# Weight sums later in VectorE's order, and the sixth down operand's difference in two parts

## The chip, the core and the metric

The kernel runs on one core of a Trainium2 chip. The time is device microseconds of one execution of the whole kernel, from inputs in HBM to the output in HBM. Five engines are named by their short names: PE (TensorE, matmuls), ACT (ScalarE), DVE (VectorE), POOL (GpSimd, here only an issuer of transfers that add to their destination) and SP (SyncE, here only an issuer of plain transfers). Every engine works through its own queue in order; they meet by semaphores.

## What is computed

A trunk of two macaron layers over 528 tokens (512 and 16 meta tokens), model width 1024, all in float32: a SwiGLU feed-forward at half weight, a mixer of gated linear attention beside grouped-query softmax attention, and a second feed-forward at half weight.

```python
def swiglu(x, w_gate, w_up, w_down):
    return (jax.nn.silu(x @ w_gate) * (x @ w_up)) @ w_down
...
    for l in range(DEPTH):
        h = h + 0.5 * swiglu(rmsnorm(h, norm_gains[l, 0]), ffn_w_gate[l, 0], ffn_w_up[l, 0], ffn_w_down[l, 0])
        h = h + mixer(rmsnorm(h, norm_gains[l, 1]), ...)
        h = h + 0.5 * swiglu(rmsnorm(h, norm_gains[l, 2]), ffn_w_gate[l, 1], ffn_w_up[l, 1], ffn_w_down[l, 1])
    return rmsnorm(h, final_norm)[:, N_META:]
```

The hidden width of the feed-forward is 2816, that is 22 tiles of 128, or 11 pairs of tiles. The change touches only the feed-forwards, of which there are four ("blocks" in the prediction).

## The kernel before

**Precision.** Every product of float32 matrices is made of three: each operand is split into a rounded part (hi) and the rest (lo), and hi*hi, hi*lo and lo*hi are summed in PSUM. For a weight slab of 128x1024 ACT makes `whi` (L287) and DVE makes `wlo` (L288); both pools have four buffers, and a slab is made three uses ahead of PE.

**Seven products instead of eight.** The feed-forward's matrices are cut in 2x2 blocks and multiplied by a Strassen-like scheme: the products "1", "2", "4" use a weight block as it lies in HBM ("11", "12", "22"), and "7", "6", "5", "3" use sums of blocks. Where a sum's two terms are both in HBM, POOL makes it by an adding transfer (L208). For the pairs from 2 to 10, DVE makes three: "7" is block 21 less block 11 (L244, in place in the tile of 21), "6" is block 22 plus "7" (L253, in place in the tile of 22), and "3" is "6" less block 12 (L256, the tile s4). Blocks "11", "12", "22" live in `wraw` (three buffers, tag raw), the sums in `wsa` and `wsb` (three each). Method `sums` issues these right after the slab of the product that it is called for has been made; `make` calls it for the products "1", "2" and "6".

**Pairs and groups.** `ffn_steps` writes out the order of the products. The 11 pairs form groups of 4, 4 and 3. The first two groups' down projection is fast too: its operands are sums of the hidden values of the group's four pairs, and its weight blocks count as pairs 11 to 14 ("quads"). When a group's last pair is nearly done, the step ("O", g, 0) makes operands "1", "2", "5" of the three finished pairs (`ks` = 0 to 2) and, after the last pair, ("O", g, 1) makes the same for pair 3 of the group and then operand "6" of all four. An operand is a hi part (ACT, L669) and a lo part (DVE, L670); a difference of hidden values (DVE, L674) comes first for "5" and "6". Operands "5" and "6" lie in the tiles tagged c, the others in g.

**Order.** The program is written in one order, and a scheduler then sets each engine's own order from readiness by its own costs. So a line that moves in the program may or may not move in an engine's queue. L614, L621 and L638 are the DVE steps that turn a pair's products into gate and up values, L648 multiplies them to hidden values, L716 adds a fast down product to h. `product_of_pair` holds the PE matmuls of L594, `fast_down` those of L708.

Of the kernel before, what the change touches and what calls it, by code (L numbers as in the profile page):

```python
# [14 lines left out]
ALU = mybir.AluOpType  # L15
# [133 lines left out]
NPAIR = FF // P // 2  # L149
# [21 lines left out]
class Weights:  # L171
# [59 lines left out]
    def sums(self, f, i, product, w):  # L231


        got, V = self.summed, self.nc.vector
        if (f, i) in OPENING and product in "12":
            (self.begin_sums if product == "1" else self.first_sum)(f, i, *[w] * (product == "1"))
        if i < 2:
            if product == "2":
                s4 = self.negative(f, i, "s4", w)
                self.add(s4, got[f, i, "6"])  # L240
                got[f, i, "3"] = s4
        elif product == "1":
            if i < NPAIR:
                V.tensor_tensor(got[f, i, "7"], got[f, i, "7"], w, ALU.subtract)  # L244
            else:
                got[f, i, "7"] = self.negative(f, i, "s3", w)
                self.add(got[f, i, "7"], self.dram(f, i, "21"))
            if not i < NPAIR:
                self.add(got[f, i, "6"], got[f, i, "7"])
        elif product == "2":  # L250
            self.kept = w
            if i < NPAIR:
                V.tensor_tensor(got[f, i, "6"], got[f, i, "6"], got[f, i, "7"], ALU.add)  # L253
        elif product == "6":
            s4 = self.long.tile([P, SLAB], F32, tag="wsa", name=f"s4_{f[0]}{f[1]}_{i}")
            V.tensor_tensor(s4, w, self.kept, ALU.subtract)  # L256
            got[f, i, "3"] = s4
# [15 lines left out]
    def make(self, upto):  # L273
        nc = self.nc
        while self.made < min(upto, len(self.loads)):
            self.fetch(self.made + 1)
            s = self.made
            load = self.loads[s]
            w = self.raws.pop(s, None)
            if w is None:  # L280
                w = self.summed.pop(load)
            hi = self.hi_pool.tile([P, SLAB], F32R, tag="whi", name=f"whi{s}")
            lo = self.lo_pool.tile([P, SLAB], F32R, tag="wlo", name=f"wlo{s}")
            for a in np.split(np.arange(SLAB), 2 if s == 0 else 1):
                cs = slice(a[0], a[-1] + 1)
                with self.tc.issue_after(self.behind) if self.behind else nullcontext():
                    nc.scalar.copy(hi[:, cs], w[:, cs])  # L287
                nc.vector.tensor_tensor(lo[:, cs], w[:, cs], hi[:, cs].bitcast(F32), ALU.subtract)  # L288
            self.got[s] = (hi, lo)
            self.got.pop(s - 12, None)  # L290
            self.made += 1
            if not isinstance(load, int) and load[2] in "126":
                self.sums(*load, w)

    def use(self, j, ahead=AHEAD_MADE):
        self.make(j + ahead)
        self.fetch(j + AHEAD_FETCHED)
        return self.got[j]

    def next(self, name):  # L300
        t = PLAN[self.pos]
        assert t[1] == name, (t, name)
        s, c = divmod(COLUMN[self.pos], SLAB)
        self.pos += 1
        hi, lo = self.use(self.at[s])
        return hi[:, c : c + t[5]], lo[:, c : c + t[5]]
# [18 lines left out]
def build(tc, ctx, xt, wts, win, par, w2, const, umask, out):  # L325
    nc = tc.nc
    V, S, G, TE = nc.vector, nc.scalar, nc.gpsimd, nc.tensor
# [24 lines left out]
    def close_pools(pools):  # L352
        for n in reversed(pools):
            slots.pop(n).release()
# [28 lines left out]
    def h(c, cs=None):  # L383
        return hall[:, c, cs or slice(0, live[0])]
# [184 lines left out]
    def ffn(l, f, norm, done, following):  # L569

        x, rs, up, n = norm.x, None, None, live[0]
        w = n // 2
# [85 lines left out]
        def operand(g, c, ks=slice(0, 4)):  # L658

            src = raw[g][{"1": 0, "2": 2, "5": 0, "6": 0, "7": 1, "3": 3, "4": 2}[c]]  # L660
            if (g, c) not in sets:
                tag = "c" if c in "56" else "g"
                sets[g, c] = [quarter(tag, F32R) for _ in range(2)]
            hi, lo = [t[:, ks] for t in sets[g, c]]
            if c == "3":
                S.activation(hi, src[:, ks], AF.Copy, scale=-1.0)
                V.scalar_tensor_tensor(lo, src[:, ks], -1.0, hi.bitcast(F32), ALU.mult, ALU.subtract)
            else:
                S.copy(hi, src[:, ks])  # L669
                V.tensor_tensor(lo, src[:, ks], hi.bitcast(F32), ALU.subtract)  # L670

        def difference(g, into, a, b, ks=slice(0, 4)):
            r = raw[g]
            V.tensor_tensor(r[into][:, ks], r[a][:, ks], r[b][:, ks], ALU.subtract)  # L674

        def operands_of(g, ks, order):
            for c in order:
                if c == "5":
                    difference(g, 0, 1, 0, ks)
                operand(g, c, ks)  # L680
# [10 lines left out]
        def fast_down(g, dq, c, part):  # L691
            last = sum(GROUPS[: g + 1]) - 1
            kinds = ("ss", "s2") if last % 2 == 0 else ("s2", "ss")
            st = made.setdefault(("S", g, dq), {})
            where = {"2": "Y", "5": "Z", "3": "Z"}.get(c, "X")
            begin = c in "125"
            if part != 2:
                if begin:
                    st[where] = pair(kinds[{"Y": 0, "Z": 1, "X": dq}[where]] == "s2")
                st["w"] = st.get("w", {})  # L700
                st["w"][c] = W.op((l, f), NPAIR + QUADS * g + dq, c, ahead=AHEAD_MADE - 1)
            acc = st[where][:, :, :w]
            hi, lo = st["w"][c]
            xs = sets[g, c]
            for k in {1: range(3), 2: range(3, 4), 3: range(4)}[part]:
                for j in range(2):
                    for i, (a, b) in enumerate(((hi, 0), (hi, 1), (lo, 0))):
                        TE.matmul(acc[:, j], a[:, j, k], xs[b][:, k], start=bool(begin and k == 0 and i == 0),  # L708
                                  stop=k == 3 and i == 2, skip_group_check=not begin)
            if part == 1:  # L710
                return
            st["w"].pop(c)
            for m, q in {"1": [(0, 0)], "2": [(0, 0)], "5": [(1, 1)], "6": [(0, 1)], "3": [(0, 1)], "7": [(1, 1)],
                         "4": [(1, 0)]}[c]:
                to = hall[:, 4 * dq + m : 4 * dq + m + 3 : 2, q * w : (q + 1) * w]
                V.tensor_tensor(to, to, acc, ALU.add)  # L716
            if dq == 1:
                sets.pop((g, c))
            operands_behind(g, dq, c)
# [24 lines left out]
        for i, step in enumerate(steps):  # L744
            if step[0] == "P":
                if step[1:] == (0, "5") and norm.acc is None:
                    for c in range(KC):
                        norm.square(c)
                product_of_pair(*step[1:])
                if step[1:] == (0, "5"):  # L750
                    rs, up = norm.rs(True)
                    W.behind = prev_act[0]
                if step[1] in (2, 3) and step[2] in "6574":
                    m = next(risen)
                    V.scalar_tensor_tensor(h(m), h(m), -1.0, up, ALU.mult, ALU.mult)
                if i == last_op:
                    close_pools(norm.pools)
                    following()
            elif step[0] == "S":
                fast_down(*step[1:])  # L760
            elif step[0] == "O":
                g, last = step[1:]
                operands_of(g, slice(3, 4) if last else slice(0, 3), "215" if last else "125")
                if last:
                    difference(g, 0, 3, 0)
                    operand(g, "6")
            else:
                down(*step[1:])
# [515 lines left out]
    for l in range(DEPTH):  # L1284
        a, b, c = norms[3 * l : 3 * l + 3]
        ffn(l, 0, a, b.chunk, lambda: operand_pools(b, "x"))
        close_pools(bp.pop())
        mixer(l, b, c.chunk_of_pair, lambda: (operand_pools(c, "xc"), bp.append(block_pools())))
        if l < DEPTH - 1:
            d = norms[3 * l + 3]  # L1290
            ffn(l, 1, c, d.pair_of, lambda: operand_pools(d, "xc"))
        else:
            ffn(l, 1, c, None, lambda: None)
# [72 lines left out]
```

## Time and profile before

| | us |
|---|---|
| median of 3 runs | 2219.3 (2217.36 to 2219.31) |
| the profiled execution | 2218.53 |
| its span, first to last instruction | 2216.8 |
| PE, DVE, ACT busy | 2164.6, 1784.4, 1210.7 |

PE is busy for nearly all of the span, so the figures of the other engines matter only where PE waits for them. In the rows, `out<-in` are tile names without buffer numbers, `<-` in square brackets names what ended the idle time before an instruction, and `q` behind an engine's name (DVEq, SPq) is its sequencer. Two instructions of DVE in a row overlap a little, so a start-to-start distance is some 0.08 us shorter than the time shown for one.

### The profile page before, as it was taken

Reading aid. Unit: us, or ns where it says so; the run is one execution under the profiler, and the core shown is the slowest. Engines: PE = TensorE matmul, PEld = TensorE weight load, DVE = VectorE, ACT = ScalarE, POOL = GpSimd, SP = SyncE. Lnnn points to the kernel's source line nnn. Section 1 sums busy time; section 2 is a strip of 40 time slices with the busy share of each in tenths; the row PEclk is TensorE's granted clock in tenths of the full one; section 3 lists DMA queues with packets and bytes.
Section 4 is the critical chain, followed back from the end, with each engine's and each line's share of the span. In section 5 each row is a group of like instructions: output and inputs, shape, how many; then the busy total and the mean of one; then the engine's idle time right before and its main releaser. Section 6 shows DMA issues by size and latency. Waiting matters only on the chain.

```text
span 2216.8 us, 40090 instructions
## 1 busy us (share of the span) xinstructions
PE 2164.6 (98%) x16506; PEld 2070.7 (93%) x16506; DVE 1784.4 (80%) x2695; ACT 1210.7 (55%) x1779; POOL 101.5 (5%) x120
## 2 busy tenths in 40 slices
PE   7999999999999999999999999999999999999998
PEld 6899999989999999999999999999788888999997
DVE  7887978486886688888789879775879767997987
ACT  7444545354785555454575445553557836554543
POOL 1000000000000001000010000000000001000100
PEclk9999999999999999999999999999999999999999
DMA  9675753212113467666566757432121146776752
GB/s 278 172 199 165 190 158 101 86 48 67 48 39 118 116 168 200 190 184 187 158 162 187 207 159 194 143 110 77 48 82 53 42 135 153 196 200 180 191 161 67
DMA packets 87463, 311.41 MB, mean 140 GB/s; under 512 B 9712, under 2 KB 12144, under 8 KB 87280
## 3 DMA queue, kind: packets, MB, share of 16 engines
q1 hardware_dynamic: 68624, 245.53, 33.0%
q0 software_dynamic: 16704, 60.82, 15.6%
q8 instruction: 130, 2.13, 0.4%
q10 hardware_dynamic: 1952, 2.50, 0.3%
q14 instruction: 53, 0.43, 0.1%
HBM read 289.94 MB, written 2.10 MB: 132 GB/s over the span
## 4 chain that ended last, share of the span: by engine, by line
PE 79%; DVE 11%; ACT 3%; issue 2%; DMA 1%; DVEq 0%; POOL 0%; ACTq 0%; POOLq 0%
PE ss L594 36%; PE mm L461 13%; PE ss L708 11%; PE ss L461 10%; PE sm L461 2%; DVE wlo L288 2%; DVE g L674 1%; PE sm L1069 1%; PE ss L1044 1%; DVE h L716 1%; PE ss L467 1%; DMA w<-win 1%; PE sm L1085 1%; ACT t L440 1%; DVE c L670 1%
## 5 line engine op out<-in xcount | busy, mean ns | idle before, releaser
L594 PE MATMUL ss<-xc,whi 128*128 128x264 f32 (+1 forms) x4928 | 905.3, 285 | 15.6 <-ACT whi L287 7.6
L594 PEld LDWEIGHTS ss<-xc,whi 128*128 128x128 f32 x4928 | 765.3, 189 | 20.5 <-ACT c L598 8.4
L594 PE MATMUL ss<-xc,wlo 128*128 128x264 f32 (+1 forms) x2464 | 701.5, 285 | 8.8 <-DVE wlo L288 8.7
L594 PEld LDWEIGHTS ss<-xc,wlo 128*128 128x128 f32 x2464 | 465.4, 189 | 11.2 <-DVE wlo L288 11.0
L288 DVE TENSOR_TENSOR wlo<-w,whi 128x1024 fp32r<-128x1024 f32 (+1 forms) x337 | 408.0, 1217 | 64.1 <-ACT whi L287 63.9
L287 ACT CAST whi<-w 128x1024 fp32r<-128x1024 f32 (+1 forms) x337 | 349.4, 1048 | 175.2 <-PE ss L594 82.1
L461 PE MATMUL mm<-x,whi 128*128 128x264 f32 (+1 forms) x1712 | 384.8, 315 | 0.0
L461 PEld LDWEIGHTS mm<-x,whi 128*128 128x128 f32 x1712 | 278.4, 188 | 16.6 <-issue 1.0
L461 PE MATMUL mm<-x,wlo 128*128 128x264 f32 (+1 forms) x856 | 266.0, 315 | 0.0
L708 PE MATMUL ss<-g,whi 128*128 128x264 f32 (+1 forms) x1280 | 238.6, 285 | 1.5 <-ACT g L669 1.4
L287 ACT CAST whi<-raw 128x1024 fp32r<-128x1024 f32 x126 | 132.1, 1048 | 163.6 <-PE mm L461 102.8
L598 ACT COPY c<-ss 128x528 f32<-128x528 f32 (+1 forms) x132 | 78.4, 594 | 259.1 <-PE ss L594 259.1
L288 DVE TENSOR_TENSOR wlo<-raw,whi 128x1024 fp32r<-128x1024 f32 x126 | 153.9, 1221 | 59.2 <-ACT whi L287 58.4
L708 PEld LDWEIGHTS ss<-g,whi 128*128 128x128 f32 x1280 | 199.0, 189 | 2.1 <-ACT g L669 1.6
L708 PE MATMUL ss<-g,wlo 128*128 128x264 f32 (+1 forms) x640 | 181.7, 284 | 0.0
L461 PEld LDWEIGHTS mm<-x,wlo 128*128 128x128 f32 x856 | 159.5, 188 | 8.5 <-issue 0.7
L461 PE MATMUL ss<-g,whi 128*128 128x264 f32 (+2 forms) x900 | 166.2, 299 | 0.0
L461 PEld LDWEIGHTS ss<-g,whi 128*128 128x128 f32 x900 | 131.7, 188 | 5.3
L208 POOL DMA_DIRECT2D w<-win x60 | 52.8, 880 | 1580.1 <-DVE wlo L288 463.9
L708 PEld LDWEIGHTS ss<-g,wlo 128*128 128x128 f32 x640 | 120.9, 189 | 0.0
L440 ACT ACTIVATE c<-c 128x528 f32<-128x528 f32 (+1 forms) x88 | 56.5, 642 | 93.6 <-DVE c L638 89.3
L708 PE MATMUL ss<-c,whi 128*128 128x264 f32 (+1 forms) x512 | 100.3, 289 | 7.1 <-DVE c L670 6.6
(267 smaller groups left out, 3375.3 us busy)
## 6 DMA issues: line engine op xcount, KB each, us to landing
w<-win SPq DMA_DIRECT2D x335, 512.0 KB, 4.5
raw<-wts SPq DMA_DIRECT2D x126, 512.0 KB, 3.3
w<-win POOLq DMA_DIRECT2D x60, 512.0 KB, 7.5
s<-win POOLq DMA_DIRECT2D x24, 512.0 KB, 7.0
w<-s POOLq DMA_DIRECT2D x24, 512.0 KB, 5.6
s<-w POOLq DMA_DIRECT2D x8, 512.0 KB, 7.7
h<-xt SPq DMA_DIRECT2D x3, 528.0 KB, 7.1
out<-h ACTq DMA_DIRECT2D x4, 256.0 KB, 2.4
```

The lines of the kernel that those rows point to most:

```text
L208: self.nc.gpsimd.dma_start(t, src, accum_op=ALU.add)
L287: nc.scalar.copy(hi[:, cs], w[:, cs])
L288: nc.vector.tensor_tensor(lo[:, cs], w[:, cs], hi[:, cs].bitcast(F32), ALU.subtract)
L440: prev_act[0] = S.activation(*args, **kw).ins
L461: TE.matmul(acc.half[i][:width], lhs, rhs[:, acc.spans[i]], start=first, stop=last)
L467: TE.matmul(a, weights, x[:, hs], start=True, stop=True)
L594: TE.matmul(acc[:, j], a[:, j, k], b[:, at], start=bool(begin and k == 0 and i == 0), stop=k == len(x) - 1 and i == 2, skip_group_check=no ...
L598: W.behind = S.copy(part(st, q), acc).ins
L670: V.tensor_tensor(lo, src[:, ks], hi.bitcast(F32), ALU.subtract)
L674: V.tensor_tensor(r[into][:, ks], r[a][:, ks], r[b][:, ks], ALU.subtract)
L708: TE.matmul(acc[:, j], a[:, j, k], xs[b][:, k], start=bool(begin and k == 0 and i == 0), stop=k == 3 and i == 2, skip_group_check=not begin)
L716: V.tensor_tensor(to, to, acc, ALU.add)
```

## The change

Three edits. In `sums`, the subtraction for "7" is issued when product "2"'s slab has been made, no longer product "1"'s; block 11's tile is kept for it (`kept1`). The addition for "6" is issued in `make`, right before the slab of "6" is made. And the difference for operand "6" is made for the three finished pairs in step ("O", g, 0) and for the last pair alone in ("O", g, 1), where it was made for all four at once.

```diff
         elif product == "1":
             if i < NPAIR:
-                V.tensor_tensor(got[f, i, "7"], got[f, i, "7"], w, ALU.subtract)
+                self.kept1 = w
...
         elif product == "2":
             self.kept = w
             if i < NPAIR:
-                V.tensor_tensor(got[f, i, "6"], got[f, i, "6"], got[f, i, "7"], ALU.add)
+                V.tensor_tensor(got[f, i, "7"], got[f, i, "7"], self.kept1, ALU.subtract)
...
             if not isinstance(load, int) and load[2] in "126":
                 self.sums(*load, w)
+            after = self.loads[s + 1] if s + 1 < len(self.loads) else 0
+            if not isinstance(after, int) and after[2] == "6" and 2 <= after[1] < NPAIR:
+                s2, s3 = [self.summed[after[:2] + (c,)] for c in "67"]
+                nc.vector.tensor_tensor(s2, s2, s3, ALU.add)
...
                 g, last = step[1:]
-                operands_of(g, slice(3, 4) if last else slice(0, 3), "215" if last else "125")
+                ks = slice(3, 4) if last else slice(0, 3)
+                operands_of(g, ks, "215" if last else "125")
+                difference(g, 0, 3, 0, ks)
                 if last:
-                    difference(g, 0, 3, 0)
                     operand(g, "6")
```

What the engines' queues make of it is shown at three places. A name such as w21_01_4 is a weight tile: block 21, layer 0, feed-forward 1, pair 4; s4 and s3 are sums, whi and wlo a slab's parts, and the last number counts buffers. Line numbers of the kernel after the change are 4 or 5 higher below the edits (L678 is the difference that was L674, L674 then is the lo part that was L670).

DVE in the second block, from the first weight slab of quad 11 to the step L621 (L625) of the group's last pair, before:

```order
L288 TENSOR_TENSOR wlo189_10090<-w11_01_11_9874,whi189_10089 128x1024
L614 TENSOR_TENSOR c816_9868<-c816_9868,ss818_10046 128x2x264
L638 TENSOR_SCALAR c816_9868<-c816_9868,rs800_9426 128x264
L288 TENSOR_TENSOR wlo190_10127<-s4_01_3_9942,whi190_10126 128x1024
L288 TENSOR_TENSOR wlo191_10162<-w12_01_11_9944,whi191_10161 128x1024
L638 TENSOR_SCALAR c816_9868<-ss814_9835,rs800_9426 128x264
L256 TENSOR_TENSOR s4_01_11_10250<-w22_01_11_9876,w12_01_11_9944 128x1024
L648 TENSOR_TENSOR g806_9504<-c816_9868,ss814_9835 128x264
L648 TENSOR_TENSOR g807_9505<-c816_9868 128x264
L288 TENSOR_TENSOR wlo192_10184<-w21_01_11_9878,whi192_10183 128x1024
L670 TENSOR_TENSOR g822_10081<-g806_9504,g821_10080 128x264
L621 TENSOR_TENSOR c815_9867<-c815_9867,ss818_10046 128x2x264
```

and after:

```order
L678 TENSOR_TENSOR g804_9504<-g807_9507,g804_9504 128x792
L618 TENSOR_TENSOR c816_9869<-c816_9869,ss818_10048 128x2x264
L288 TENSOR_TENSOR wlo190_10130<-s4_01_3_9944,whi190_10129 128x1024
L642 TENSOR_SCALAR c816_9869<-c816_9869,rs800_9428 128x264
L288 TENSOR_TENSOR wlo191_10165<-w12_01_11_9946,whi191_10164 128x1024
L642 TENSOR_SCALAR c816_9869<-ss814_9836,rs800_9428 128x264
L288 TENSOR_TENSOR wlo192_10187<-w21_01_11_9879,whi192_10186 128x1024
L652 TENSOR_TENSOR g806_9506<-c816_9869,ss814_9836 128x264
L652 TENSOR_TENSOR g807_9507<-c816_9869 128x264
L256 TENSOR_TENSOR s4_01_11_10253<-w22_01_11_9877,w12_01_11_9946 128x1024
L674 TENSOR_TENSOR g822_10083<-g806_9506,g821_10082 128x264
L625 TENSOR_TENSOR c815_9868<-c815_9868,ss818_10048 128x2x264
```

The early part of the difference (792 columns) stands right behind wlo189 (not repeated), and the weight sum s4 has moved from ahead of wlo192 to behind it. Eleven rows below L621 the difference of 128x1056 is one of 128x264. The other seven groups show the same.

DVE at the pair that follows that group, before and after:

```order
L288 TENSOR_TENSOR wlo200_10478<-w11_01_4_10252,whi200_10477 128x1024
L244 TENSOR_TENSOR w21_01_4_10254<-w21_01_4_10254,w11_01_4_10252 128x1024
L716 TENSOR_TENSOR h_82<-h_82,ss825_10160 128x2x264
L288 TENSOR_TENSOR wlo201_10508<-w21_01_12_10017,whi201_10507 128x1024
L716 TENSOR_TENSOR h_82<-h_82,ss830_10312 128x2x264
L288 TENSOR_TENSOR wlo202_10540<-w12_01_4_10351,whi202_10539 128x1024
L253 TENSOR_TENSOR w22_01_4_10256<-w22_01_4_10256,w21_01_4_10254 128x1024
```

```order
L288 TENSOR_TENSOR wlo200_10481<-w11_01_4_10255,whi200_10480 128x1024
L720 TENSOR_TENSOR h_82<-h_82,ss825_10163 128x2x264
L288 TENSOR_TENSOR wlo201_10510<-w21_01_12_10019,whi201_10509 128x1024
L720 TENSOR_TENSOR h_82<-h_82,ss830_10315 128x2x264
L288 TENSOR_TENSOR wlo202_10542<-w12_01_4_10354,whi202_10541 128x1024
L253 TENSOR_TENSOR w21_01_4_10257<-w21_01_4_10257,w11_01_4_10255 128x1024
L297 TENSOR_TENSOR w22_01_4_10259<-w22_01_4_10259,w21_01_4_10257 128x1024
```

The subtraction (L244, now L253) has moved past two wlo and two additions to h; the addition (L253, now L297) has stayed. On SP the load of pair 5's block 11, which takes the buffer of pair 4's, has moved behind that of pair 5's block 22.

POOL's adding transfers at the first group of the first block, before:

```order
L208 DMA s3_00_11_1133<-win 128x1024
L208 DMA w22_00_11_916<-s3_00_11_1133 128x1024
L208 DMA w21_00_11_918<-win 128x1024
L208 DMA s3_00_12_1263<-win 128x1024
L208 DMA w22_00_12_1055<-s3_00_12_1263 128x1024
```

and after:

```order
L208 DMA s3_00_11_1134<-win 128x1024
L208 DMA w21_00_11_917<-win 128x1024
L208 DMA w22_00_11_915<-s3_00_11_1134 128x1024
L208 DMA s3_00_12_1264<-win 128x1024
L208 DMA w22_00_12_1055<-s3_00_12_1264 128x1024
```

The sum w21 of quad 11 has moved ahead of w22<-s3. In the other groups POOL's order is the same before and after.

## The prediction

> **What bounds the kernel now.** I read the page first, then the list of waits for TensorE (PE), then the chain of work that ended last at one of the eight places that the change touches, and VectorE's (DVE) timeline there.
>
> ```profile
> span 2216.8 us, 40090 instructions
> PE 2164.6 (98%) x16506; PEld 2070.7 (93%) x16506; DVE 1784.4 (80%) x2695; ACT 1210.7 (55%) x1779; POOL 101.5 (5%) x120
> ...
> PE ss L594 <- DVE wlo L288: 8.7, 8, 3.1
> ...
> PE ss L708 <- DVE c L670: 6.6, 8, 0.9
> ...
> PE ss L708 <- ACT g L669: 1.4, 1, 1.4
> ...
> PE ss L708 <- DVE wlo L288: 0.6, 1, 0.6
> ```
>
> PE is busy for 98% of the span, so time can only come from the few microseconds in which it waits (columns: us in total, times, longest). One line is this change's own: PE waits eight times, 0.9 us at most and 6.6 in all, for the low part of an operand in a c tile (L670). That is the sixth down operand, once for each of two groups in four feed-forward blocks.
>
> How such a wait comes about is in the chain at the place of the second block's first group. The timelines of PE, ACT (ScalarE) and DVE at the same place follow it.
>
> ```profile
> 867.13 2.94 PE ss L594 x24
> 870.09 0.71 DVE c L621
> ...
> 877.70 1.25 DVE g L674
> 878.96 1.23 DVE h L716 x2
> 880.18 1.24 DVE c L670
> ```
>
> ```profile
> 881.47 0.39 PE L708 MATMUL ss<-c,whi 128*128 128x264 f32 x1 [0.91 <-DVE c L670]
> ```
>
> ```profile
> 877.00 1.05 ACT L287 CAST whi<-s 128x1024 fp32r<-128x1024 f32 x1
> 879.04 1.08 ACT L669 CAST c<-g 128x1056 fp32r<-128x1056 f32 x1 [1.00 <-DVE g L674]
> ```
>
> ```profile
> 859.98 0.98 DVE L670 TENSOR_TENSOR c<-g,c 128x792 fp32r<-128x792 f32 x1
> 860.87 1.22 DVE L288 TENSOR_TENSOR wlo<-w,whi 128x1024 fp32r<-128x1024 f32 x1
> ...
> 870.09 0.70 DVE L621 TENSOR_TENSOR c<-c,ss 128x528 f32<-128x528 f32 x1 [1.01 <-PE ss L594]
> ```
>
> PE's product ends at 870.07 and lets DVE start at L621. From there DVE has work without a pause until the difference (L674, four pairs wide) at 877.70; ACT rounds it (879.04 to 880.12), DVE takes the rest of the rounding (L670), and PE, which was ready 0.91 us before, goes on at 881.47. Just ahead of L621, DVE had been idle for 1.01 us.
>
> **The change, part by part.** *The difference in two parts.* The widths and durations of L674 in all of the trace are these:
>
> ```profile
> L674 DVE TENSOR_TENSOR g<-g,g 128x1056 f32<-128x1056 f32 x18 | 22.6, 1254 | 0.2
> L674 DVE TENSOR_TENSOR g<-g,g 128x1024 f32<-128x1024 f32 x6 | 7.3, 1221 | 0.1
> L674 DVE TENSOR_TENSOR g<-g,g 128x792 f32<-128x792 f32 x6 | 5.9, 983 | 0.2
> L674 DVE TENSOR_TENSOR g<-g,g 128x264 f32<-128x264 f32 x6 | 2.6, 433 | 0.2
> ...
> L674 DVE TENSOR_TENSOR g<-g,g 128x256 f32<-128x256 f32 x2 | 0.8, 424 | 0.1
> ```
>
> On the chain the wide instruction becomes a narrow one: 1.254 - 0.433 = 0.82 us less at the six places with 528 columns, 1.221 - 0.424 = 0.80 at the two of the last block. The same steps with that number: L674 ends at 877.70 + 0.43 = 878.13; ACT is free from 878.05 and starts 0.09 after L674's end, as before, at 878.22, and ends at 879.30; the two h adds (1.23 together) fit in between; L670 runs from 879.33 to 880.59; PE goes on at 880.65. It is ready at 881.47 - 0.91 = 880.56, so 0.82 of the 0.91 is gained, and 0.09 stays.
>
> The price is the early part, 0.98 us long, which pushes what follows by 0.9 (start to start after the row of that width above, 859.98 to 860.87). It stands right after the wlo of 860.87, ahead of the idle 1.01 us before L621, so that idle time hides it with 0.1 to spare. If that cover were gone, L621 would start up to 0.9 late and the gain of that place would be eaten; that is the bound on this side. Between these two points the order also moves a weight sum (L256, s4) behind the next wlo; that swaps two instructions of the same length, and the wlo is then ready sooner. In the last block the idle time is shorter:
>
> ```profile
> 1950.03 0.69 DVE L621 TENSOR_TENSOR c<-c,ss 128x512 f32<-128x512 f32 x1 [0.57 <-PE ss L594]
> ```
>
> Only 0.57 is idle here, so at the last block's two places L621 may come 0.3 late, 0.6 in all; the new order also puts a wlo behind each small instruction whose result the next one reads, which fills pauses, so I take none of it. Sum of this part: 6 x 0.82 + 2 x 0.80 = 6.5 us, with 0 (no cover) and 8 x 0.91 = 7.3 as its ends. I take 6.5, since the first of PE's waits for L670 aside, all are 0.9 and show the same steps.
>
> *The opening.* The eighth place, in the first group of the first block, looks different. The rows by stretch (columns: length, then busy time and count of PE, PEld, DVE, ACT, POOL, then PE clock, DMA share, GB/s) compare it with the next group's, from the same PE instruction to the same one, and give the stretch at half clock:
>
> ```profile
> 105.06:127.72 22.66, 20.27 (x145) 19.43 (x145) 18.28 (x27) 12.33 (x15) 2.60 (x3) 0.92 0.93 221
> 233.74:253.22 19.48, 18.47 (x145) 17.87 (x145) 18.19 (x27) 12.83 (x16) 2.60 (x3) 1.00 0.88 222
> ...
> 120.80:124.20 3.40, 3.40 (x18) 3.40 (x17) 3.40 (x5) 2.81 (x4) 0.87 (x1) 0.50 1.00 231
> ```
>
> The same 145 matmuls take 3.18 us more: waits of 1.4 and 0.6 us (the third and fourth wait quoted first) and a stretch in which PE got half its clock. The cause is in the chain there, with GpSimd's (POOL) timeline under it:
>
> ```profile
> 102.42 10.05 DMA w<-win
> ...
> 112.58 1.05 ACT whi L287
> ```
>
> ```profile
> 92.03 0.86 POOL L208 DMA_DIRECT2D s<-win  x1 [13.32 <-ACT s L203]
> 101.79 0.88 POOL L208 DMA_DIRECT2D w<-s  x1 [8.90 <-issue]
> ```
>
> The adding transfer that makes the quad's operand "5" (w21) is issued at 102.42 and lands at 112.5; ACT's whi at 112.58 waits for it, and with it DVE and PE. It was issued so late only because POOL's queue is in order: ahead of it stood w22<-s3, which waits for s3 (issued at 92.03) until 101.79. In the changed order w21 stands ahead of w22<-s3. Its own condition is its base load, which SP issues here:
>
> ```profile
> 91.74 0.33 SPq L198 DMA_DIRECT2D w<-win  x1
> ```
>
> ```profile
> w<-win SPq DMA_DIRECT2D x4, 512.0 KB, 4.1
> w<-win POOLq DMA_DIRECT2D x1, 512.0 KB, 7.9
> ```
>
> By the landing times of 4.1 and, for an adding one, 7.9 to 10.05 us (the two rows are of a later stretch, 900 to 910), the base is there at about 96 and the sum at 104 to 106, well ahead of 112.5; ACT could take it when it is next free, and PE would not wait. Then this place runs as the next group's does: 3.2 us gained, beside the 0.82 already counted. The cost that goes with it: w22<-s3 is issued behind w21, at 101.8 as before, since s3 still lands then, and with 7.9 us is there at 109.7; its first reader, s4 (L256), stands in DVE's new order just ahead of L621, at about 111 if the place runs as the second group's does. Ends: 0 (the transfer lands late all the same) and 3.2.
>
> Half clock, row first: in 3.40 us PE did 18 matmuls, where at 18.47 / 145 = 0.127 us they take 2.3; 1.1 of the 3.18 us is the clock's, and I count it as gone with the waits. [...]
>
> *The weight sums.* The list of DVE's waits has
>
> ```profile
> DVE w L244 <- DMA w<-win: 33.4, 16, 5.1
> ```
>
> but the order shows that the scheduler leaves nearly all of these subtractions and additions where they were. Pair 3's addition moves by a few rows in the first and third block, which I cost at nothing, since its reader comes four wlo later. Otherwise they move past other work only for the pair that follows a group (pairs 4 and 8, eight times): the subtraction goes from behind wlo of "11" to behind wlo of "12". There it did not wait before, and PE does not wait in that stretch, so nothing is gained. What it costs: "11" keeps its slot of three (wraw) longer, and its next user, the load of pair 5's "11", is SP's, with what is queued behind it.
>
> ```profile
> 897.31 1.22 DVE L244 TENSOR_TENSOR w<-w,w 128x1024 f32<-128x1024 f32 x1
> ...
> 900.81 1.22 DVE L288 TENSOR_TENSOR wlo<-w,whi 128x1024 fp32r<-128x1024 f32 x1
> ...
> 910.53 1.22 DVE L244 TENSOR_TENSOR w<-w,w 128x1024 f32<-128x1024 f32 x1
> ...
> 915.18 1.22 DVE L288 TENSOR_TENSOR wlo<-w,whi 128x1024 fp32r<-128x1024 f32 x1 [1.69 <-ACT whi L287]
> ```
>
> ```profile
> 898.60 0.33 SPq L198 DMA_DIRECT2D w<-win  x1
> ```
>
> The load went out at 898.60, right after the subtraction's end (898.53). The rows up to the wlo of 900.81 move up by one place and the subtraction takes that one's, 900.81 to 902.03, so the load goes out 3.5 us later. With 4.1 us to land it is there at 906.2, and its first reader that could suffer is the next subtraction, at 910.53: covered by 4 us. Cost 0; ends 0 and what the rival below gives.
>
> The extra eight DVE instructions (0.983 + 0.433 - 1.254 = 0.16 us each) lie in the same cover. Sum: 6.5 + 3.2 = 9.7 us. The profiled execution took 2218.53 us (span 2216.8 and 1.7 around it), 0.8 below the median of the runs, 2219.3; I take the sum off the median: 2209.6 us.
>
> **The rivals.** *The opening keeps its wait* (w21 lands late, beside s3 on the same queue): seven places give 5 x 0.82 + 2 x 0.80 = 5.7, and the eighth no more than its own wait there:
>
> ```profile
> 127.74 0.39 PE L708 MATMUL ss<-c,whi 128*128 128x264 f32 x1 [0.33 <-DVE c L670]
> ```
>
> That is 5.7 + 0.3 = 6.0, so 2213.3. For it: s3 alone took from 92.03 to 101.79. Against: between the base's landing (96) and the need (112.5) lie 16 us, and an adding transfer took 7.9 to 10.05. 0.20.
>
> *The half clock stays*: the stretch from 120.80 has another cause than the waits just ahead of it, and comes back: 9.7 - 1.1 = 8.6, so 2210.7. For it: the 3.1 us wait set none off. Against: among all such places it stands only where PE waited twice in 4 us. 0.08. [...]
>
> *The early part is not hidden*: DVE reaches L621 0.9 late at each place, which eats the 0.82; what is left is 3.2 - 8 x (0.9 - 0.82) = 2.6, so 2216.7. For it: the spare is 0.1 us. Against: the sum of the rows. 0.10.
>
> *Slower: the held slot.* The late load of pair 5's "11", with SP's later loads behind it, reaches the subtraction at 910.53 with its full 3.5 us. DVE's next pause is 1.69 us (before 915.18); what is over, 1.8 us, goes through wlo to PE, at eight places: 14.4 - 9.7 = 4.7 slower, so 2224.0. It decides from the point where the loads land more than 8 us after 902.0; those of that stretch took 4.1. 0.12.
>
> **How the numbers follow.** The forecast has 0.50: 2209.6. From no change the measurement can tell about 0.2%, 4.4 us. Faster by more: the forecast, the half clock and most of the first rival, 0.50 + 0.08 + 0.17 = 0.75. Within: the rest of it and the third, 0.13. Slower: 0.12. The range reaches up to the third rival, 2217.0, and down to 2206.5: all of 7.3, 3.2, and some 2 of the 8.7 us of waits for wlo in the opening, where the order has small shifts that I count at nothing.
>
> **What would show it.** Right: the wait for c at L670 falls from 6.6 us to under 1; L621 still starts within 0.1 us of its PE product at seven places; POOL's w21 of the first group goes out near 96 and ACT's whi no longer waits for it; no stretch at half clock before 130 us; the first group's stretch is as long as the second's. Wrong: new waits of PE on wlo in the 20 us behind a group, or DVE waiting at L253 of pair 5 for a load; or L621 starting late.

## The result, and the profile after

The changed kernel takes 2210.99 us (median of 6 runs, 2209.06 to 2213.69) against 2219.47 for the kernel before (6 runs on the same chip, 2217.36 to 2221.5): ratio 0.9961, with a 95% interval from 0.995 to 0.9972. That is 8.5 us less, between 6.2 and 11.1. The profiled execution took 2211.05, its span is 2209.2.

The page's first lines and the list of waits for TensorE (us in total, times, longest) answer to the four waits shown of before:

```profile
span 2209.2 us, 40079 instructions
PE 2162.4 (98%) x16506; PEld 2070.2 (94%) x16506; DVE 1785.4 (81%) x2703; ACT 1214.1 (55%) x1779; POOL 101.8 (5%) x120
...
PE ss L598 <- DVE wlo L288: 8.8, 8, 3.1
...
PE ss L712 <- DVE c L674: 3.4, 8, 0.6
```

The waits for ACT's g (1.4) and for wlo (0.6) behind the first group are gone. The wait for the sixth operand's low part is halved, from 6.6 to 3.4 us, not gone as forecast; yet the gain per place is as forecast. The place of the second block's first group shows why. DVE, ACT and PE there:

```profile
867.18 0.70 DVE L625 TENSOR_TENSOR c<-c,ss 128x528 f32<-128x528 f32 x1 [0.24 <-PE ss L598]
...
874.79 0.43 DVE L678 TENSOR_TENSOR g<-g,g 128x264 f32<-128x264 f32 x1
875.13 1.31 DVE L720 TENSOR_TENSOR h<-h,ss 128x528 f32<-128x528 f32 x2
876.42 1.26 DVE L674 TENSOR_TENSOR c<-g,c 128x1056 fp32r<-128x1056 f32 x1
```

```profile
875.31 1.08 ACT L673 CAST c<-g 128x1056 fp32r<-128x1056 f32 x1 [0.16 <-DVE g L678]
```

```profile
877.73 0.39 PE L712 MATMUL ss<-c,whi 128*128 128x264 f32 x1 [0.39 <-DVE c L674]
```

From L625 to the difference it is 874.79 - 867.18 = 7.61 us, as before (877.70 - 870.09); from there everything is 0.83 earlier: PE goes on 877.73 - 867.18 = 10.55 us behind L625, where it was 881.47 - 870.09 = 11.38. But PE is ready at 877.34, 10.16 behind L625, where it was 10.47. So 0.83 was gained and 0.39 is still waited for, since PE itself came 0.31 sooner.

The same gain by stretch (length, then busy time and count of PE, PEld, DVE, ACT, POOL, then PE clock, DMA share, GB/s), from the same PE instruction to the same one: first group, second group, the group above, and the two of the last block; then the last three of before.

```profile
106.92:125.58 18.66, 18.24 (x145) 17.82 (x145) 18.17 (x28) 12.32 (x15) 2.61 (x3) 1.00 0.85 215
231.56:250.20 18.64, 18.16 (x145) 17.73 (x145) 18.18 (x28) 12.33 (x15) 2.61 (x3) 1.00 0.87 218
...
859.06:877.71 18.65, 18.20 (x145) 17.78 (x145) 18.17 (x28) 12.33 (x15) 2.61 (x3) 1.00 0.91 224
1936.28:1954.61 18.33, 17.66 (x145) 17.26 (x145) 18.01 (x28) 12.43 (x16) 2.63 (x3) 1.00 0.86 225
2057.35:2075.54 18.19, 17.62 (x145) 17.21 (x145) 17.95 (x28) 12.43 (x16) 2.62 (x3) 1.00 0.89 225
```

```profile
861.97:881.45 19.48, 18.50 (x145) 17.90 (x145) 18.19 (x27) 12.70 (x16) 2.60 (x3) 1.00 0.89 218
1942.14:1961.16 19.02, 18.02 (x145) 17.40 (x145) 18.11 (x27) 12.59 (x16) 2.62 (x3) 1.00 0.89 225
2064.12:2083.11 18.99, 17.97 (x145) 17.33 (x145) 18.11 (x27) 12.59 (x16) 2.61 (x3) 1.00 0.88 225
```

PE's busy time falls by 0.30 to 0.36 as well, with the same 145 matmuls. Before, the matmul that reads the operand's hi part came late too: it started 0.05 behind ACT's end at 880.12 (879.04 + 1.08), without being listed as a wait. After the change it stands two matmuls earlier in PE's order and starts 0.42 behind ACT's end at 876.39 (875.31 + 1.08), so it is no longer held up. These are its rows, before and after:

```profile
880.17 0.39 PE L708 MATMUL ss<-c,whi 128*128 128x264 f32 x1
```

```profile
876.81 0.29 PE L712 MATMUL ss<-c,whi 128*128 128x264 f32 x1
```

The sum of the gains is 22.66 - 18.66 = 4.0 for the first group, 5 x 0.83 for the other five with 528 columns, 0.69 and 0.80 for the last block: 9.6 us.

The opening shows what was expected of GpSimd's queue and of ACT behind it:

```profile
93.94 0.86 POOL L208 DMA_DIRECT2D s<-win  x1 [13.92 <-ACT s L203]
96.54 0.88 POOL L208 DMA_DIRECT2D w<-win  x1 [1.74 <-DMA w<-win]
102.34 0.88 POOL L208 DMA_DIRECT2D w<-s  x1 [4.91 <-DVE g L674]
```

```profile
110.05 1.06 ACT L287 CAST whi<-w 128x1024 fp32r<-128x1024 f32 x1 [0.30 <-PE ss L598]
```

But the spans differ by 7.6 us, not 9.6. The missing 2 us were lost ahead of the first group, where the order of every engine is still nearly the same. These rows are, before and after, the same 215 matmuls (from 42 us on), and of after the wait and the two stretches at half clock in them:

```profile
42.21:75.01 32.80, 26.90 (x215) 26.19 (x214) 23.99 (x31) 16.13 (x20) 1.75 (x2) 1.00 0.58 167
```

```profile
41.72:76.87 35.15, 29.64 (x215) 29.01 (x214) 24.58 (x32) 16.24 (x20) 1.76 (x2) 0.90 0.64 183
...
53.40:56.82 3.42, 3.24 (x14) 3.25 (x15) 3.42 (x5) 0.65 (x1) 0.07 (x1) 0.50 0.86 290
70.47:73.88 3.41, 3.41 (x17) 3.30 (x16) 3.41 (x5) 0.42 (x1) 0.00 (x0) 0.50 0.15 36
```

```profile
53.58 0.59 PE L598 MATMUL ss<-xc,wlo 128*128 128x264 f32 x1 [3.15 <-DVE wlo L288]
```

Whether the change made that stretch 2.35 us longer, or chance did, was the first open question; the second, which edit is worth what.

### The profile page after: what moved, and what is told of

Same layout as the page of the kernel before. It is cut to its first block, busy times and chain, and to the rows that moved or that the text cites. A ratio compares the mean times of both kernels' runs of the same rounds, so it can differ in the third digit from the quotient of the medians.

```text
span 2209.2 us, 40079 instructions
## 1 busy us (share of the span) xinstructions
PE 2162.4 (98%) x16506; PEld 2070.2 (94%) x16506; DVE 1785.4 (81%) x2703; ACT 1214.1 (55%) x1779; POOL 101.8 (5%) x120
## 4 chain that ended last, share of the span: by engine, by line
PE 81%; DVE 11%; ACT 4%; issue 2%; DMA 2%; SPq 0%; DVEq 0%; ACTq 0%
PE ss L598 37%; PE mm L465 13%; PE ss L712 11%; PE ss L465 10%; PE sm L465 2%; DVE wlo L288 2%; DMA w<-win 2%; PE sm L1074 1%; PE ss L1049 1%; DVE g L678 1%; ACT whi L287 1%; PE sm L1090 1%; DVE h L720 1%; PE ss L471 1%; PE sm L1091 1%
## 5 line engine op out<-in xcount | busy, mean ns | idle before, releaser
L598 PEld LDWEIGHTS ss<-xc,wlo 128*128 128x128 f32 x2464 | 466.5, 189 | 11.1 <-DVE wlo L288 10.9
L465 PE MATMUL ss<-g,wlo 128*128 128x264 f32 (+2 forms) x450 | 106.2, 300 | 0.0
```

The source lines that it names most:

```text
L465: TE.matmul(acc.half[i][:width], lhs, rhs[:, acc.spans[i]], start=first, stop=last)
L598: TE.matmul(acc[:, j], a[:, j, k], b[:, at], start=bool(begin and k == 0 and i == 0), stop=k == len(x) - 1 and i == 2, skip_group_check=no ...
```

## The experiments

All times are medians with the ratio to runs of the kernel before on the same chip, whose medians there were 2220.57, 2221.07 and 2220.64 us.

**The parts alone.** The difference in two parts, without the weight sums' edits:

```diff
-                operands_of(g, slice(3, 4) if last else slice(0, 3), "215" if last else "125")
+                ks = slice(3, 4) if last else slice(0, 3)
+                operands_of(g, ks, "215" if last else "125")
+                difference(g, 0, 3, 0, ks)
                 if last:
-                    difference(g, 0, 3, 0)
```

> Only the difference in two parts; the weight sums stand as before. Theory of the prediction: the terms add up, and GpSimd's order does not change with this edit. Seven places give 0.7 to 0.84 us each and the opening's place no more than its own 0.33 us: 5.7 to 6.2 us, so about 2213.5 against 2219.5. In the trace GpSimd's transfer that makes w21 of quad 11 still goes out near 102.4 us, ScalarE's whi still waits for it, and the stretch at half clock from about 121 us stays. Rival: the early part is paid for in the opening, where the changed kernel lost some 1.9 us before 105 us (the wait at the wlo of 53 us grew from 1.3 to 3.2 us): then that loss shows here too, and 4 us are left, 2215.5.

Measured: 2215.2 us, ratio 0.9978 (0.9969 to 0.9987): 4.9 us gained, 2.9 to 6.9. PE's waits for the sixth operand are those of the whole change, and the first group's stretch is as long as before, at half clock in part:

```profile
PE ss L708 <- DVE c L670: 3.4, 8, 0.5
PE ss L708 <- ACT g L669: 2.6, 1, 2.6
```

```profile
105.83:128.68 22.85, 20.09 (x145) 19.46 (x146) 18.35 (x28) 11.68 (x15) 2.60 (x3) 0.93 0.91 227
```

So this edit does what its term says, and nothing for the first group. The rival's 2215.5 lies in the interval too, but its mechanism isn't in the trace: the wait at the wlo near 53 us is 1.9 us there and not 3.2, and the 215 matmuls of the opening took 34.2 us, between before and after. The second trace of the kernel before (under the repeats below) has 3.35 us at that wlo without any edit.

The later subtraction alone:

```diff
         elif product == "1":
             if i < NPAIR:
-                V.tensor_tensor(got[f, i, "7"], got[f, i, "7"], w, ALU.subtract)
+                self.kept1 = w
...
             if i < NPAIR:
+                V.tensor_tensor(got[f, i, "7"], got[f, i, "7"], self.kept1, ALU.subtract)
                 V.tensor_tensor(got[f, i, "6"], got[f, i, "6"], got[f, i, "7"], ALU.add)
```

> Only the subtraction for the operand of product 7 is issued later (with product 2, and the addition right behind it). Theory of the prediction: the held slot costs nothing, 2219.5 as before, with pair 5's load 3.5 us later and no new wait of TensorE. Rival (held slot): the late load reaches the next subtraction, 2221 or more. Rival (opening): the loss of 1.9 us before 105 us comes from this edit, 2221.4.

Measured: 2220.16 us, ratio 0.9998 (0.9989 to 1.0007). The held slot costs nothing that can be told. Its trace also has the first group without a stretch at half clock, though w21 still goes out behind w22<-s3:

```profile
105.75:126.52 20.77, 19.09 (x145) 18.06 (x145) 18.20 (x27) 12.68 (x16) 2.60 (x3) 1.00 0.91 223
```

Counted from the stretch's first matmul, w21 goes out 1.8 us earlier here than in the trace of before, so PE waits less as well, and 22.66 - 20.77 = 1.9 us is not the price of the clock alone. That price can be read from the same 24 matmuls without any wait in them, before and after the change:

```profile
120.61:124.69 4.08, 4.08 (x24) 4.08 (x22) 4.04 (x6) 3.40 (x4) 0.87 (x1) 0.58 0.99 225
```

```profile
119.65:122.49 2.84, 2.82 (x24) 2.61 (x22) 2.84 (x4) 2.55 (x4) 0.00 (x0) 1.00 0.95 224
```

The clock's share of the 3.18 us is 4.08 - 2.84 = 1.24, and 1.9 are left for the waits.

The later addition alone:

```diff
-                V.tensor_tensor(got[f, i, "6"], got[f, i, "6"], got[f, i, "7"], ALU.add)
+                pass
...
                 self.sums(*load, w)
+            after = self.loads[s + 1] if s + 1 < len(self.loads) else 0
+            if not isinstance(after, int) and after[2] == "6" and 2 <= after[1] < NPAIR:
+                s2, s3 = [self.summed[after[:2] + (c,)] for c in "67"]
+                nc.vector.tensor_tensor(s2, s2, s3, ALU.add)
```

> Only the addition for the operand of product 6 is issued later; this is the edit that puts w21 of quad 11 ahead of w22 on GpSimd's queue. Theory of the prediction: 3.2 us less, 2216.3; the transfer goes out near 96 us, no half clock near 121 us, and the eight waits for the low part of the sixth operand stay at 0.9 us (the one of the opening comes up to that too). Rival: the loss before 105 us comes from this edit, so that 1.3 us are left, 2218.2. Rival: the order on GpSimd's queue alone is not enough, the wait in the opening stays, 2219.5.

Measured: 2218.26 us, ratio 0.999 (0.9981 to 0.9999): 2.2 us gained, 0.2 to 4.2. The first group's stretch is now that of the second group before the change (19.48), with w21 out first and ACT not waiting for it:

```profile
109.81:129.29 19.48, 18.56 (x145) 17.94 (x145) 18.18 (x27) 12.78 (x16) 2.60 (x3) 1.00 0.82 216
```

```profile
99.50 0.88 POOL L208 DMA_DIRECT2D w<-win  x1 [1.80 <-DMA w<-win]
105.00 0.87 POOL L208 DMA_DIRECT2D w<-s  x1 [4.63 <-DVE g L674]
```

The three parts give 4.9 + 0.4 + 2.2 = 7.5 us, the whole 8.5; they add up within their intervals. The rival's 2218.2 fits the time as well; the repeats below settle it.

**GpSimd's queue alone.** The two transfers exchanged by hand, no row moved on any other engine (`add` returns its instruction for this, and `first_sum` keeps that of quad 11 in the first block as `ahead`):

```diff
-                self.add(got[f, i, "6"], got[f, i, "7"])
+                with self.tc.issue_after(self.ahead) if (f, i) == ((0, 0), NPAIR) else nullcontext():
+                    self.add(got[f, i, "6"], got[f, i, "7"])
```

> The kernel before, with one pair of rows exchanged on GpSimd's queue and nothing else on any engine: the adding transfer that makes w21 of quad 11 stands ahead of the one that adds s3 to w22. Theory that this order is what the late addition brought: the transfer goes out near 97 us, the stretch of the first group falls from 22.7 (with a stretch at half clock) or 20.8 (without one, as in the trace with the late subtraction alone) to 19.5 us; 1.3 to 3.2 us gained, 0.06 to 0.14%. Rival: VectorE's order there is needed too, the stretch stays at 20.8 or more, nothing gained.

Measured: 2217.13 us, ratio 0.9987 (0.9977 to 0.9996): 2.9 us gained, 0.9 to 5.1, by two rows on a queue that is busy for 5% of the span. The times don't tell this from the late addition's 2.2 us, but the traces do: the stretch is 20.43, not 19.5:

```profile
95.66 0.88 POOL L208 DMA_DIRECT2D w<-win  x1 [3.23 <-DVE g L651]
101.37 0.87 POOL L208 DMA_DIRECT2D w<-s  x1 [4.83 <-DVE g L677]
```

```profile
108.93 1.06 ACT L203 ACTIVATE s<-w 128x1024 f32<-128x1024 f32 x1 [2.48 <-DMA w<-win]
109.89 1.03 ACT L290 CAST whi<-w 128x1024 fp32r<-128x1024 f32 x1
```

ACT no longer waits for w21, but for the load that the instruction ahead of it in its queue reads (s3 of the next quad, 2.48 us). With the late addition that wait is at most 0.3 us in the seven traces that have it. SP issues this load 2.80 us ahead of the stretch's first matmul in all thirteen traces of this document, so it is not a matter of its slot; it lands 7.1 us after its issue here, 7.8 in the other trace with the exchange by hand (the last run below) and 4.3 to 4.9 in the seven. So the order on GpSimd's queue is worth 2.2 of the 3.2 us in the traces, and the late addition brings the other 0.9. Since both traces with the exchange by hand show that wait and none of the seven does, it is hardly chance. What makes the load slower without it, other transfers beside it perhaps, is not shown.

**Repeats.** The changed kernel and the kernel before once more, for their traces of the opening, and the changed kernel timed again.

> The changed kernel once more, for its trace of the opening. Theory that the opening's length is chance (one load's landing and whether the clock is halved): the stretch that took 27.4 us between 50 and 75 us may come out anywhere from 24 to 30. Rival that the late addition makes it long: 27 us or more again.

> The kernel before once more, for its trace of the opening. Theory: w21 of quad 11 is issued near 102 us again and the first group's stretch is 20.5 us or more, with or without a stretch at half clock near 121 us; what lies ahead of it, 32.8 us between 42 and 75 us the first time, comes out anywhere from 32 to 38. Rival: the stretch can come out at 19.5 us in this order as well, and the first trace was an unlucky one.

> The changed kernel again, timed on the same chip as the next run. By the first comparison 8.5 us below the kernel before (0.9961), by the sum of two stretches in the traces 2.1 to 4.0 us for the first group and 5.6 for the other seven places, 7.7 to 9.6.

Measured: 2208.83 us for the one run of the changed kernel, 2219.95 for that of the kernel before; timed again the changed kernel takes 2209.81 us, ratio 0.9954 (0.9941 to 0.9968), so 10.2 us gained, 7.1 to 13.1; the 7.7 to 9.6 expected lie in that interval. The 215 matmuls of the opening, changed kernel and kernel before, and the first group of the latter with its stretch at half clock:

```profile
41.90:74.23 32.33, 28.33 (x215) 27.70 (x214) 24.58 (x32) 16.23 (x20) 1.76 (x2) 0.95 0.68 190
```

```profile
107.03:129.47 22.44, 20.43 (x145) 19.40 (x145) 18.28 (x27) 12.14 (x15) 2.61 (x3) 0.92 0.97 228
123.00:126.41 3.41, 3.41 (x17) 3.22 (x16) 3.41 (x5) 2.87 (x3) 0.87 (x1) 0.50 1.04 208
41.69:76.99 35.30, 28.43 (x215) 27.72 (x214) 24.06 (x31) 16.12 (x20) 1.76 (x2) 0.95 0.56 155
```

The lengths have changed places: 35.15 and then 32.33 for the changed kernel, 32.80 and then 35.30 for the one before. So the 2 us by which the profile fell short are chance. Over all thirteen traces the opening takes 32.0 to 38.1 us, with no order that keeps it at one end. The first group's stretch is not chance: with w21 late, 22.66, 22.44, 22.85 and 20.77; with w21 first, 18.1 to 20.43 in nine traces, none of them with half clock there.

**Cover.** The seventh operand's difference in two parts too, whose early part finds almost no idle time left:

```diff
-                difference(g, 1, 1, 3)
+                difference(g, 1, 1, 3, slice(3, 4))
...
                 difference(g, 0, 3, 0, ks)
+                if not last:
+                    difference(g, 1, 1, 3, ks)
```

> The changed kernel, and the seventh operand's difference in two parts as well, with its early part (128x792) beside the other one. VectorE's early part is another 0.98 us ahead of the step that reads the group's last pair, where only 0.23 us of idle time is left in the changed kernel's trace at the first block's second group; its late part is 0.82 us shorter. Theory that cover decides: that step comes 0.75 us late at each of eight places, the 0.82 us shorter instruction stands behind what TensorE waits for, so about 0.4 to 0.75 us lost per place, 2214 to 2217 against 2211. Rival: the scheduler's new order hides it (a weight sum or a wlo moves behind that step), the remaining wait of 0.4 us goes away, 3 us gained: 2208.

Measured: 2215.78 us, ratio 0.998 (0.9971 to 0.9989): 4.8 us slower than the changed kernel by the medians, 4.2 by the two ratios. DVE at the first block's second group, that stretch, and a line of the list of PE's waits that the changed kernel doesn't have:

```profile
241.59 0.70 DVE L625 TENSOR_TENSOR c<-c,ss 128x528 f32<-128x528 f32 x1
242.39 1.23 DVE L288 TENSOR_TENSOR wlo<-w,whi 128x1024 fp32r<-128x1024 f32 x1
243.53 0.70 DVE L642 SCALAR_TENSOR_TENSOR c<-c,rs 128x528 f32<-128x528 f32 x1
```

```profile
233.25:252.19 18.94, 18.57 (x145) 17.96 (x145) 18.23 (x28) 12.20 (x15) 2.60 (x3) 1.00 0.85 205
```

```profile
PE ss L712 <- ACT c L673: 3.5, 8, 1.2
```

L625 now follows its predecessor without a pause, and in the scheduler's new order the wlo of 1.2 us that stood behind L642 stands ahead of it. L625 is 0.2 us late against its PE product at six places and 0.45 in the last block, not 0.75. The place takes 0.3 us more than after the change, not less, and so do the five others with 528 columns; the two of the last block take 0.8 and 0.9 more, where PE waits 1.2 us for the hi part: 3.4 us in all. The same trick that pays while 1.01 us are idle costs when 0.24 are. How much of the loss is L625's lateness and how much the new place of the wlo, these runs don't tell apart.

**What was left of the wait.** In the changed kernel's rows an h add and a wlo (0.70 and 1.22 us) stand ahead of the small difference. Here they are put behind it:

```diff
-                difference(g, 0, 3, 0, ks)
-                if last:
-                    operand(g, "6")
+                if not last:
+                    difference(g, 0, 3, 0, ks)
+                else:
+                    with tc.high_priority():
+                        difference(g, 0, 3, 0, ks)
+                        operand(g, "6")
```

> The changed kernel, with the last pair's difference and the sixth operand ahead of the waiting weight slab and h additions in VectorE's and ScalarE's queues. Theory: what is left of the wait (0.39 us at six places, 0.55 at two) comes from the 1.2 and 0.7 us instructions that stood ahead of the small difference; it goes, 3.4 us gained against the changed kernel, 2207.6 against 2211. Rival: wlo of the same product, now 0.4 us later, or the whi that moves behind the operand on ScalarE takes its place: nothing gained, 2211, with new waits of TensorE on wlo or whi behind the group.

> The changed kernel with the late part of the difference and the sixth operand first, timed beside the changed kernel. Theory from its trace (stretch of a group 18.65 to 18.10 us at six places, 18.3 to 17.55 at two): 6 x 0.55 + 2 x 0.75 = 4.8 us below the changed kernel, about 12.5 to 13 below the kernel before. Rival: what is gained there is lost elsewhere (the earlier run gave 11.6 below the kernel before, which leaves 3.1): 2 us or less below the changed kernel.

Measured: 2209.43 us, ratio 0.9948 (0.9935 to 0.996), and beside the changed kernel on one chip 2207.85 (2206.79 to 2208.75) against 2209.81 (2209.55 to 2212.78). It beats the changed kernel by 2.0 us by the medians and 2.7 by the ratios (0.9942 against 0.9954), not by the 3.4 to 4.8 expected; by the medians the second rival's "2 us or less" holds as well. The wait for c is gone and a group's stretch falls to 18.1 (17.5 in the last block), but a new wait shows, for the low part of the last operand ("4"):

```profile
PE ss L712 <- DVE g L674: 0.4, 2, 0.2
```

```profile
2083.06 0.39 PE L712 MATMUL ss<-g,whi 128*128 128x256 f32 x1 [0.21 <-DVE g L674]
```

```profile
2080.05 1.22 DVE L288 TENSOR_TENSOR wlo<-w,whi 128x1024 fp32r<-128x1024 f32 x1
2081.19 0.68 DVE L720 TENSOR_TENSOR h<-h,ss 128x512 f32<-128x512 f32 x1
2081.79 1.22 DVE L674 TENSOR_TENSOR g<-g,g 128x1024 fp32r<-128x1024 f32 x1
```

DVE works without a pause up to that operand, so PE, now earlier, waits for it there. What was lost is no wlo or whi, as the rival had it, but DVE's queue as a whole. Only the two places of the last block are long enough to be listed, but at all eight the matmul that reads this operand starts 0.04 us after its low part is done. The eight stretches are 4.7 us shorter than in the trace of the changed kernel timed beside it; counted up to this matmul, 3.3 us of that are left.

**Without the weight sums' edits.** The same with the two rows exchanged on GpSimd's queue by hand and the weight sums as before the change (the diffs are those of the two runs above, on the kernel before).

> The difference in two parts, its late part first as in the run before, and GpSimd's two rows exchanged, but the weight sums of VectorE where they were before the change. Theory that the weight sums' move is worth only what it did on GpSimd's queue: the same time as the run before, 2207.6. Rival: the late addition has a price in the opening (between 50 and 75 us on the kernel before's clock the three traces with it took 27.4, 28.4 and 30.2 us, the three without it 25.0, 26.4 and 24.2): then this is 2 to 4 us faster than the run before, 2205.

Measured: 2209.29 us, ratio 0.9953 (0.994 to 0.9965), by the medians the same as the run above on the same chip (2209.43). But the first group's stretch is not the same. Here and in the run above it takes:

```profile
105.64:126.02 20.38, 18.59 (x145) 17.96 (x146) 17.62 (x27) 11.47 (x15) 2.60 (x3) 1.00 0.82 206
```

```profile
104.42:122.52 18.10, 18.06 (x145) 17.85 (x146) 17.60 (x27) 11.80 (x15) 2.60 (x3) 1.00 0.83 207
```

The other seven agree to 0.01 us. A difference of 2.3 us can't be told from five runs of each (2208.22 to 2211.89 here, 2206.54 to 2210.47 above), so the equal medians don't bear out the theory, and the traces speak against it: the exchange of two transfers gives a part of what the weight sums' edits are worth, and the late addition the rest. The rival's price of the late addition in the opening doesn't show either (34.1 us here, 32.0 above).

## Why the prediction was right

Its forecast was 2209.6 us, the runs gave 2210.99 and 2209.81, and its two terms are the ones that the parts show. That it comes so close is in part luck: the opening alone differs by 6 us from one execution to another.

- **The difference in two parts, 6.5 us at eight places.** Right in size: 0.83 at the five places with 528 columns outside the opening (0.82 forecast), 0.69 and 0.80 in the last block (0.80 each). Alone it gave 4.9, where the prediction's own count without the opening is 5.7 to 6.0.
- **Its cover.** Right: L625 has 0.24 us of idle time left where 0.1 was reckoned, at six places. In the last block it has none; the stretch there that gained 0.69 in place of 0.80 bounds its lateness at 0.1, where up to 0.3 was allowed. The cover is as thin as reckoned: in the changed kernel's second trace ACT waits 1.40 us for a load at 1208.92, at the third block's first group; there L625 starts 0.5 late, and the stretch is 19.13 in place of 18.63.
- **"The wait falls from 6.6 to under 1".** Wrong: 3.4. PE was taken to be ready as late as before (880.56), and it was ready 0.31 earlier, because the matmul of the hi part had been held up without being listed. The gain is not the wait that went but the stretch that got shorter.
- **The opening, 3.2 us.** Right in size, 22.66 to 18.66 with the 0.82 in it, and so are its halves: 1.24 for the clock where 1.1 was reckoned, 1.9 for the waits where it was 2.1. Its cause was right for 2.2 of it, by the exchange of two rows alone; the other 0.9 came only with the late addition itself (20.43 against 19.48), for which the prediction had no term.
- **The weight sums, 0.** Right for the subtraction, 0.9998; for the addition see the 0.9 above. The rival of the held slot (2224) is out: pair 5's subtraction (L253) starts at 906.85 us in the changed kernel's trace with no idle time ahead of it.
- **The other rivals.** The opening did not keep its wait, and the half clock near 121 us did not come back in nine traces. The sign "no stretch at half clock before 130 us" failed all the same, with the two at 53 and 70 us, which come and go in the opening. The early part was hidden; that it costs when it isn't is shown by the place where the cover ran out (19.13 for 18.63) and, with a moved wlo beside it, by the run with a second early part.
- **The low end, 2206.5,** counted on shorter waits for wlo in the opening. They come out at 6.9 to 11.5 us in all, by chance; 2206.5 was too hopeful as an effect of the change.

## What to carry to other kernels

A wait of the bound engine says how late one instruction was, not how much the place can gain: compare the length of the same stretch from the same instruction to the same one, since small hold-ups that are listed nowhere go or come with it (here the listed wait fell by 0.52 us and the place gained 0.83). An operation split so that its early part falls into an idle stretch pays only as long as that stretch lasts (0.83 us gained per place where 1.01 us were idle, 0.3 lost by the next split where 0.24 were); read the idle time in front of the step that follows, and stop when it is used up. A queue that only issues transfers can hold back the bound engine for microseconds with two rows in the wrong order (2.2 us in the traces here), and its busy share, 5% of the span here, does not show it.

## What the runs showed of the hardware

**Half clock comes and goes.** The five rows of stretches at half clock in this document are 3.40 to 3.42 us long: from 120.80 and 123.00 in the two traces of the kernel before, from 53.40 and 70.47 in the changed kernel's, from 572.92 in that of the difference split alone. The length of one wait of PE does not decide it. In the changed kernel's trace PE waits 3.15 us before 53.58 and 2.36 before 69.34, and the clock is at half from 53.40 and from 70.47. In that of the kernel before PE waits 3.13 and 1.44 us, and no half clock stands ahead of 120.80:

```profile
67.46 0.39 PE L594 MATMUL ss<-xc,wlo 128*128 128x264 f32 x1 [3.13 <-DVE wlo L288]
...
72.10 0.39 PE L594 MATMUL ss<-xc,wlo 128*128 128x264 f32 x1 [1.44 <-DVE wlo L288]
```

So about the same wait goes with half clock in one execution and not in another, which is a part of the opening's spread: its 215 matmuls keep PE busy for 29.64 us with the two stretches and for 26.90 with none. The prediction counted the stretch near 121 us as gone with its waits, and the runs bear that out as a count: three of the four traces with w21 late have it, none of the nine with w21 first. What sets a stretch off is not shown.

**A stretch with no wait.** In four traces a stretch at half clock stands near 570 us, in the mixer, where PE does not wait but works on matmuls with few columns, 2 and 16 (this is the one of the kernel with the difference split alone). It costs 1.4 us: 300 matmuls around it take 38.9 us in the four traces and 37.5 to 37.6 in the others.

```profile
572.92:576.33 3.41, 3.41 (x18) 3.34 (x18) 2.91 (x9) 2.08 (x4) 0.00 (x0) 0.50 0.01 2
```

What sets it off in these four traces and not in the nine others is not shown.

**A load's landing.** The same load, pair 2's block 21, issued near 42 us in the same order on SP's queue, was used by DVE at 49.21 in the trace of the kernel before and at 52.45 in that of the later addition alone. From issue to landing it took 6.9 us in the former and 10.7 in the latter, each time with two of GpSimd's adding transfers beside it, and 6.4 to 10.7 us in the thirteen traces.
